# One-core two-layer hybrid encoder: moving loads, copies and token updates at the border between the layers

## The chip, the cores and the metric

The kernel runs on one core of a Trainium2 chip. The metric is the device time of one execution in microseconds; the median of the runs is quoted. Engines: TensorE (PE) multiplies, VectorE (DVE) and ScalarE (ACT) do elementwise work, GpSimd (POOL) does small work and issues stores, SyncE (SP) issues loads. Each engine works through its own queue in order.

## The reference

Two layers of a hybrid block over 512 tokens of width 2048, in float32:

```
h = rmsnorm(x, g_pre)
z = h @ w_in                     # 2048 -> 7184 columns: GLA q,k,v,gate,alpha and attention q,k,v,gate
o_gla = gated linear attention (4 heads, chunk 64), rmsnorm per head, * silu(gate)
o_att = chunked attention with relative bias (8 heads), rmsnorm per head, * silu(gate)
y = concat(o_gla, o_att) @ w_out # 2048 -> 2048
x = x + rmsnorm(y, g_post)
```

The change touches the end of the first layer's output projection (`w_out`), the update of `x`, and the start of the second layer's input projection.

## The kernel before

**Matrix products.** Weights are cut into blocks of 512 columns. A float32 product is made of three products of parts: each operand is split into a high part and the rest, and high times high, high times low and low times high are added up. For a weight chunk (128 x 1024) `Job.high` makes the high part with a ScalarE cast (line 202, tile `wh`, four buffers), `Job.low` the low part with a VectorE subtraction (line 211, tile `wl`, three buffers). Token operands are split in the same way (lines 105 and 106).

The gate blocks (`AG0`, `AG1`) are multiplied directly (`std_gemm`, line 311): eight chunks, and for two token tiles 12 matmuls per chunk. All other blocks are multiplied in pairs by a seven-product scheme (`fast_gemm`, lines 379 and 389): products P1 to P7 with four chunks each, 12 matmuls per chunk. Their weights are sums of quarter blocks built in a tile `H`: P1 takes H as loaded, P5, P6 and P4 add a loaded `raw` chunk to H (line 196), P7 takes H minus a chunk (line 198), P2 and P3 take `raw` chunks. The output projection consists of the pairs W01 and W23; their order is `PROD_END`: P1 and P2 alternately, then P5 and P6, P3, P7, P4.

**Preparing ahead.** All chunks of both layers stand in one list. After each chunk `ahead()` issues loads up to five, casts and low parts up to four chunks ahead. A scheduler with a model of the engines turns the program into one queue per engine; `tc.issue_after(i)` ties the instructions in its block behind instruction i, where both stand on the same engine. `last_load`, `last_h`, `last_cast`, `last_low` are the latest load, H load, cast and low part.

**The border.** `project` (line 1317) takes the outputs of a product, squares them on ScalarE with a running sum (line 1330), and multiplies them with the gain `g_post` on VectorE (line 1334, or 1343 for W01's, late). For W01's last product P4 it first copies them from the accumulator (line 1328). When one half of the tokens is complete, `finish_both` (line 1368) reduces the squares, takes the power -1/2 on POOL (line 431), and updates x: z = y * r + x, on VectorE (line 1386), each stored to `x_mid` by POOL. The first half is complete after P7 of W23, the second after P4. `prep_half` then squares the new rows (line 444), reduces (445), takes the power, scales the rows (ScalarE line 499, VectorE line 501), transposes them on TensorE (515), evacuates with the next layer's gain (526), and splits them into operands `a11c`, `a12c` and others.

The old x rows are loaded by `Tokens.load` (line 459) a piece at a time from `residual`, during W23. Updates of the second half stand behind chosen splits (`half_lows`), and P4's sums in W23 of the first layer behind chosen updates (`half_adds`).

Of the kernel before, what the change touches and what calls it, by code (L numbers as in the profile page):

```python
# [16 lines left out]
L = 2  # L17
S = 512
D = 2048
# [14 lines left out]
def hybrid_trunk(  # L34
# [104 lines left out]
    class Job:  # L139
# [14 lines left out]
        def load(self):  # L154
            k, c, p, b0, b1 = self.kind, self.c, self.pair, self.b0, self.b1
            end = b0 >= NB_IN and k != "std"
            if end:
                c = OC[c]
            top, bottom = (c + 4, c) if end else (c, c + 4)
            if k == "std":  # L160
                self.raw = self.fetch(rtile("raw", bufs=5), b0, c)
            elif k == "P1":
                p["H", self.c] = self.fetch(rtile("H"), b0, top)
                last_h[0] = last_load[0]
            elif k == "P5":
                p["r", self.c] = self.fetch(rtile("raw", bufs=5), b1, top)
            elif k == "P6":
                p["r", self.c] = self.fetch(rtile("raw", bufs=5), b1, bottom)
            elif k == "P7":
                p["r", self.c] = p.pop(("t", self.c), None) or self.fetch(rtile("raw", bufs=5), b0, top)  # L170
            elif k == "P2" or (k == "P4" and end):
                p["r", self.c] = self.fetch(rtile("raw", bufs=5), b0, bottom)
            sums = (so_d if end else sa_d)[self.l]
            src = sums.get((LEFT.get(k), c))
            if src is not None and b0 != NB_IN and not (k == "P5" and b0 == AV0):
                until(lambda: k == "P4" or (id(sums), LEFT[k], c) in written)
                self.a = rtile("sa", (2, 512), F32R)
                last_load[0] = nc.sync.dma_start(flat(self.a), src).ins
            if k == "P5" and b0 == W23[0] and self.l == L - 1:
                with tc.issue_after(last_h[0]):  # L180
                    p["t", self.c] = self.fetch(slot(SPARE[self.c], [2, 512]), b0, c + 4)

        def high(self):
# [3 lines left out]
            else:  # L187
                h, r = p["H", c], p.get(("r", c))
                src = h if k in ("P1", "P5", "P6", "P4") else r
                with ExitStack() as ties:  # L190
                    if self.b0 >= NB_IN:
                        ties.enter_context(tc.issue_after(lows[-2]))
                    if k == "P4" and self.l < L - 1 and self.b0 == W23[0]:
                        ties.enter_context(tc.issue_after(half_adds[3 if self.c else 1]))
                    if k in ("P5", "P6") or (k == "P4" and self.b0 >= NB_IN):
# [288 lines left out]
    full = {}  # L484
    half_adds, half_lows, half_turns, half_rows = [], [], [], [None]

# [236 lines left out]
    def layer(l):  # L723
# [595 lines left out]
        def project(o, n, src, gp=None, comb=None, between=None):  # L1319
# [6 lines left out]
            y = src if comb is None else comb(dst if gp is None else t2())  # L1326
            if gp is None and comb is None:
                nc.scalar.copy(dst, src)
            j = t2(dtype=BF16)
            nc.scalar.activation(j, y, AF.Square, scale=D ** -0.5, accum_out=ssy[o][:, n : n + 1])  # L1330
            if between is not None:
# [38 lines left out]
        def finish_both(pair, xs):  # L1370
# [6 lines left out]
            yield  # L1377
            n = 0
            for j in range(2):
                t, c0 = 2 * pair + j, 0  # L1380
                for z in xs[j]:
                    wd = z.shape[-1]
                    yt = ys[t, c0 // 1024][:, c0 % 1024 : c0 % 1024 + wd]
                    with tc.issue_after(half_lows[3 + n // 2]) if pair else nullcontext():
                        half_adds.append(
                            nc.vector.scalar_tensor_tensor(
                                out=z, in0=yt, scalar=r[:, j : j + 1], in1=z, op0=ALU.mult, op1=ALU.add
                            ).ins
                        )
                    nc.gpsimd.dma_start(x_mid[t * P : (t + 1) * P, c0 : c0 + wd], z)  # L1390
                    n, c0 = n + 1, c0 + wd
                    if c0 % 1024 == 0:
                        yield

# [47 lines left out]
        def residual(k, c):  # L1442
# [71 lines left out]
```

## Time and profile before

| | |
|---|---|
| median of 3 runs (lowest, highest) | 1627.13 us (1626.03, 1629.71) |
| profiled execution: its own time, its span | 1630.47 us, 1628.4 us |
| TensorE, weight load, VectorE, ScalarE, POOL busy | 1605.2, 1374.1, 1271.8, 919.2, 128.9 us |
| mean granted TensorE clock | 0.996 |
| read from and written to device memory | 377.02 MB, 61.62 MB; 269 GB/s over the span |

W23 of the first layer starts at 728 us of the span, its P4 at 795, the second layer at 813. In the rows of instructions the first number is the start in us from the start of the span, the second the time from the start of the first to the end of the last instruction of the row, "x3" their count, and in brackets the engine's idle time before it and what ended that. Waits are in us in total, how often, and the longest. In the stretches, each engine has its busy time and instructions; then come the granted TensorE clock, the DMA engines' busy share and GB/s.

### The profile page before, as it was taken

What the parts mean: (1) busy time and instruction counts of PE and PEld (TensorE: products, weight loads), DVE (VectorE), ACT (ScalarE), POOL (GpSimd) and SP (SyncE); (2) the same over time, 40 slices, a digit from 0 to 9 for tenths busy, and PEclk for the clock granted to TensorE, in tenths of its full rate; (3) what the DMA queues carried; (4) which work ended last, traced back from release to release, by engine and by line L of the source; (5) the groups of instructions that cost most, each with busy time, mean ns of one, the idle gap of its engine ahead of it and who ended that gap; (6) DMA issues with size and microseconds to landing.
All of it is one profiled execution on the core that took longest, in us unless ns stands there. A gap on an engine that the chain in (4) does not pass through costs nothing.

```text
span 1628.4 us, 24480 instructions
## 1 busy us (share of the span) xinstructions
PE 1605.2 (99%) x8938; PEld 1374.1 (84%) x8938; DVE 1271.8 (78%) x1646; ACT 919.2 (56%) x1507; POOL 128.9 (8%) x192
## 2 busy tenths in 40 slices
PE   9999999999999999999989999999999999999997
PEld 7887999998888778878778889999988887788886
DVE  5987778678677868988878677686786778689887
ACT  7544445566555556665686444456574555565644
POOL 0120000010000010100122000000100100101001
PEclk9999999999999999999999999999999999999999
DMA  9697686785868768697879976866958677686887
GB/s 370 235 386 265 239 296 209 230 304 175 278 215 296 249 227 302 229 345 262 305 240 336 377 248 247 285 229 223 314 212 282 214 282 267 219 305 239 330 301 196
DMA packets 133928, 438.17 MB, mean 269 GB/s; under 512 B 14404, under 2 KB 27204, under 8 KB 133776
## 3 DMA queue, kind: packets, MB, share of 16 engines
q1 hardware_dynamic: 117072, 375.99, 66.4%
q0 software_dynamic: 16160, 59.53, 9.9%
q8 instruction: 71, 1.16, 0.3%
q10 hardware_dynamic: 576, 1.08, 0.2%
q14 instruction: 49, 0.40, 0.1%
HBM read 377.02 MB, written 61.62 MB: 269 GB/s over the span
## 4 chain that ended last, share of the span: by engine, by line
PE 89%; DVE 3%; DMA 3%; issue 2%; ACT 1%; POOL 0%; DVEq 0%; SPq 0%; POOLq 0%; ACTq 0%
PE mm L389 49%; PE mm L379 20%; PE mm L311 8%; PE ax L939 2%; PE ax L389 2%; DMA raw<-in_w_dram 1%; PE ax L1125 1%; PE ax L922 1%; DVE wl L211 1%; PE ax L1097 1%; PE ax L902 1%; PE ax L901 1%; PE ax L900 1%; DMA H<-in_w_dram 1%; DMA S<-g 1%
## 5 line engine op out<-in xcount | busy, mean ns | idle before, releaser
L389 PE MATMUL mm<-wh,sa 128*128 128x512 f32 x1600 | 518.0, 394 | 1.8 <-DMA sa<-S 0.9
L211 DVE TENSOR_TENSOR wl<-H,wh 128x1024 fp32r<-128x1024 f32 x256 | 312.1, 1220 | 98.7 <-PE mm L389 31.7
L202 ACT CAST wh<-H 128x1024 fp32r<-128x1024 f32 x256 | 268.4, 1051 | 212.0 <-PE mm L389 89.7
L389 PEld LDWEIGHTS mm<-wh,sa 128*128 128x128 f32 x1600 | 299.4, 188 | 74.6 <-issue 9.7
L202 ACT CAST wh<-raw 128x1024 fp32r<-128x1024 f32 (+1 forms) x237 | 248.5, 1052 | 200.9 <-PE mm L389 90.4
L211 DVE TENSOR_TENSOR wl<-raw,wh 128x1024 fp32r<-128x1024 f32 (+1 forms) x237 | 287.6, 1216 | 68.1 <-PE mm L389 27.1
L389 PE MATMUL mm<-wl,sa 128*128 128x512 f32 x800 | 312.6, 391 | 0.3 <-DVE wl L211 0.3
L379 PE MATMUL mm<-sa,wh 128*128 128x256 f32 x1280 | 237.4, 285 | 0.0
L389 PE MATMUL mm<-wh,a 128*128 128x512 f32 x640 | 211.5, 394 | 2.1 <-ACT wh L202 2.1
L379 PEld LDWEIGHTS mm<-sa,wh 128*128 128x128 f32 x1280 | 200.2, 191 | 0.3
L379 PE MATMUL mm<-sa,wl 128*128 128x256 f32 x640 | 181.1, 283 | 0.0
L389 PEld LDWEIGHTS mm<-wl,sa 128*128 128x128 f32 x800 | 150.3, 188 | 30.3 <-DVE wl L211 0.7
L196 DVE TENSOR_TENSOR H<-H,raw 128x1024 f32<-128x1024 f32 x144 | 174.9, 1219 | 1.0
L389 PEld LDWEIGHTS mm<-wh,a 128*128 128x128 f32 x640 | 119.3, 188 | 27.7 <-ACT wh L202 2.9
L389 PE MATMUL mm<-wl,a 128*128 128x512 f32 x320 | 125.7, 393 | 0.0
L379 PEld LDWEIGHTS mm<-sa,wl 128*128 128x128 f32 x640 | 122.5, 191 | 0.3 <-DVE wl L211 0.2
L198 DVE TENSOR_TENSOR raw<-H,raw 128x1024 f32<-128x1024 f32 x60 | 73.5, 1224 | 51.9 <-DMA raw<-in_w_dram 51.6
L431 POOL TENSOR_TENSOR sm<-sm,mhalf 128x2 f32<-128x2 f32 (+2 forms) x40 | 53.0, 1324 | 762.5 <-DVE sm L949 459.2
L389 PE MATMUL mm<-wh,g 128*128 128x512 f32 x320 | 101.7, 391 | 1.5 <-ACT ev L341 1.2
L379 PE MATMUL mm<-a,wh 128*128 128x256 f32 x512 | 95.4, 285 | 0.0
L341 ACT COPY ev<-mm 128x512 f32<-128x512 f32 x104 | 60.8, 585 | 60.6 <-PE mm L389 43.9
L217 DVE TENSOR_TENSOR H<-H,raw 128x1024 f32<-128x1024 f32 x48 | 58.7, 1224 | 38.2 <-DMA raw<-in_w_dram 38.1
(247 smaller groups left out, 2316.2 us busy)
## 6 DMA issues: line engine op xcount, KB each, us to landing
raw<-in_w_dram SPq DMA_DIRECT2D x315, 512.0 KB, 5.2
sa<-S SPq DMA_DIRECT2D x184, 512.0 KB, 4.4
H<-in_w_dram SPq DMA_DIRECT2D x64, 512.0 KB, 5.1
sa<-A SPq DMA_DIRECT2D x48, 512.0 KB, 5.8
S<-g POOLq DMA_DIRECT2D x32, 512.0 KB, 9.6
sa<-oS SPq DMA_DIRECT2D x32, 512.0 KB, 5.5
oS<-g POOLq DMA_DIRECT2D x16, 512.0 KB, 4.5
oS<-sa POOLq DMA_DIRECT2D x16, 512.0 KB, 5.7
```

The costliest lines, as they stand in the source:

```text
L196: nc.vector.tensor_tensor(out=h, in0=h, in1=r, op=ALU.add)
L198: nc.vector.tensor_tensor(out=r, in0=h, in1=r, op=ALU.subtract)
L202: last_cast[0] = nc.scalar.copy(self.wh[:, z, :], src[:, z, :]).ins
L211: last_low[0] = nc.vector.tensor_tensor(out=self.wl[:, z, :], in0=self.src[:, z, :], in1=self.wh[:, z, :].bitcast(F32), op=ALU.subtract).ins
L217: nc.vector.tensor_tensor(out=h, in0=h, in1=self.src, op=ALU.add)
L311: nc.tensor.matmul(pss[o], a(part, kk, o) if callable(a) else a[:, part, t], rhs[:, kk, :], start=(i == 0 and kk == 0 and m == 0), stop=(i ...
L341: nc.scalar.copy(e, src[t])
L379: nc.tensor.matmul(dst, lhs[:, kk, f], a[:, part, tok], start=(fresh and kk == 0 and m == 0 and ft % 2 == 0), stop=(c == 3 and kk == 1 and ...
L389: last_mm[0] = nc.tensor.matmul(out_ps[t], a[:, part, tok], rhs[:, kk, :], start=(fresh and kk == 0 and m == 0), stop=(c == 3 and kk == 1 ...
L431: nc.gpsimd.tensor_tensor(out=out_r, in0=v, in1=mhalf[:, : v.shape[-1]], op=ALU.pow)
L900: nc.tensor.matmul(ps[:, :n], self.qh[:, t], self.kh[:, :n], start=True, stop=False)
L939: nc.tensor.matmul(o, self.pt[i][:, j * P : (j + 1) * P], av[hd // 4, j // 2][:, j % 2, (hd % 4) * P : (hd % 4 + 1) * P], start=(j == 0), ...
```

## The change

Five edits, all at the end of an output projection.

1. `finish_both`: the second half's six updates are tied behind the latest low part (`last_low`) instead of behind chosen splits, and the task yields after each update (before: after each full row piece of 1024 columns). The list `half_adds` goes.
2. `high`: P4's sums in the first layer's W23 are no longer tied behind updates.
3. `residual`: x loads are tied behind the latest H load instead of the latest load of any kind. Operand loads (`sa`) of W23 in the first layer (`mid`) are tied behind the latest H load too.
4. `load`: in the first layer's W23, P7's own chunks are fetched when P6 is prepared, into the slots `a110` to `a113`, which hold P1's operands until P1 is done. Before, they were fetched into the `raw` ring when P7 was prepared. The second layer has an early fetch already, at P5.
5. `project`: the ScalarE copies (and squares) of W01's P4 are tied behind the latest cast.

```diff
@@ load
+            mid = end and b0 == W23[0] and self.l < L - 1
...
             if src is not None and b0 != NB_IN and not (k == "P5" and b0 == AV0):
                 until(lambda: k == "P4" or (id(sums), LEFT[k], c) in written)
                 self.a = rtile("sa", (2, 512), F32R)
-                last_load[0] = nc.sync.dma_start(flat(self.a), src).ins
-            if k == "P5" and b0 == W23[0] and self.l == L - 1:
+                with tc.issue_after(last_h[0]) if mid else nullcontext():
+                    last_load[0] = nc.sync.dma_start(flat(self.a), src).ins
+            if b0 == W23[0] and k == ("P6" if mid else "P5"):
                 with tc.issue_after(last_h[0]):
-                    p["t", self.c] = self.fetch(slot(SPARE[self.c], [2, 512]), b0, c + 4)
+                    p["t", self.c] = self.fetch(slot(f"a11{self.c}" if mid else SPARE[self.c], [2, 512]), b0, c + 4)
@@ high
-                with ExitStack() as ties:
-                    if self.b0 >= NB_IN:
-                        ties.enter_context(tc.issue_after(lows[-2]))
-                    if k == "P4" and self.l < L - 1 and self.b0 == W23[0]:
-                        ties.enter_context(tc.issue_after(half_adds[3 if self.c else 1]))
+                with tc.issue_after(lows[-2]) if self.b0 >= NB_IN else nullcontext():
@@ project
-            if gp is None and comb is None:
-                nc.scalar.copy(dst, src)
             j = t2(dtype=BF16)
-            nc.scalar.activation(j, y, AF.Square, scale=D ** -0.5, accum_out=ssy[o][:, n : n + 1])
+            with tc.issue_after(last_cast[0]) if gp is None and comb is None else nullcontext():
+                if gp is None and comb is None:
+                    nc.scalar.copy(dst, src)
+                nc.scalar.activation(j, y, AF.Square, scale=D ** -0.5, accum_out=ssy[o][:, n : n + 1])
@@ finish_both
-            n = 0
...
-                    with tc.issue_after(half_lows[3 + n // 2]) if pair else nullcontext():
-                        half_adds.append(
-                            nc.vector.scalar_tensor_tensor(
-                                out=z, in0=yt, scalar=r[:, j : j + 1], in1=z, op0=ALU.mult, op1=ALU.add
-                            ).ins
+                    with tc.issue_after(last_low[0]) if pair else nullcontext():
+                        nc.vector.scalar_tensor_tensor(
+                            out=z, in0=yt, scalar=r[:, j : j + 1], in1=z, op0=ALU.mult, op1=ALU.add
                         )
                     nc.gpsimd.dma_start(x_mid[t * P : (t + 1) * P, c0 : c0 + wd], z)
-                    n, c0 = n + 1, c0 + wd
-                    if c0 % 1024 == 0:
-                        yield
+                    c0 += wd
+                    yield
@@ residual
-                xs[half].load(last_load[0], 1)
+                xs[half].load(last_h[0], 1)
```

The queues that come out differ in the first layer's W23 and the first blocks of the second layer, and in a few places at the second layer's W23. Line numbers of the changed kernel are one to three lower than before (the low part is at 209, the update at 1383).

**Start of W23, first layer.** ScalarE's queue; `g8` and `g11` take W01's last outputs from the accumulators `mm_1266` and `mm_1267`, `H_1373` and `H_1387` are P1's first two chunks, `raw_1384` and `raw_1390` P2's. Before:

```order
L1330 ACTIVATE t2_1378_7199,ssy_1376_7195<-g8_1377_7197 128x512
L1330 ACTIVATE t2_1381_7205,ssy_1379_7201<-g11_1380_7203 128x512
L1328 COPY g8_1377_7197<-mm_1266_6621 128x512
L1330 ACTIVATE t2_1394_7280,ssy_1376_7195<-mm_1266_6621 128x512
L202 CAST wh_1383_7221<-H_1373_7189 128x1024
L202 CAST wh_1386_7239<-raw_1384_7223 128x1024
L1328 COPY g11_1380_7203<-mm_1267_6622 128x512
```

Now:

```order
L200 CAST wh_1383_7221<-H_1373_7189 128x1024
L1329 ACTIVATE t2_1378_7199,ssy_1376_7195<-g8_1377_7197 128x512
L1329 ACTIVATE t2_1381_7205,ssy_1379_7201<-g11_1380_7203 128x512
L200 CAST wh_1386_7239<-raw_1384_7223 128x1024
L200 CAST wh_1389_7257<-H_1387_7241 128x1024
L200 CAST wh_1392_7275<-raw_1390_7259 128x1024
L1328 COPY g8_1377_7197<-mm_1266_6621 128x512
```

The four casts of the first two P1 and P2 chunks stand ahead of the copies. On SP's queue, before, the H loads stand among operand loads (`sa`) and x loads (`g16`, `g17`, `g12`):

```order
L178 DMA sa_1428_7421<-oS202_128 128x1024
L151 DMA raw_1390_7259<-in_w_dram 128x1024
L459 DMA g17_1422_7396<-in_x_dram 128x1024
L151 DMA raw_1404_7309<-in_w_dram 128x1024
L151 DMA H_1373_7189<-in_w_dram 128x1024
L178 DMA sa_1432_7444<-oS100_122 128x1024
L459 DMA g12_1423_7397<-in_x_dram 128x1024
L151 DMA raw_1412_7349<-in_w_dram 128x1024
L151 DMA H_1387_7241<-in_w_dram 128x1024
L151 DMA raw_1415_7369<-in_w_dram 128x1024
L151 DMA H_1393_7277<-in_w_dram 128x1024
L151 DMA H_1409_7330<-in_w_dram 128x1024
```

Now:

```order
L151 DMA H_1373_7189<-in_w_dram 128x1024
L151 DMA raw_1412_7349<-in_w_dram 128x1024
L151 DMA H_1387_7241<-in_w_dram 128x1024
L151 DMA raw_1415_7369<-in_w_dram 128x1024
L151 DMA H_1393_7277<-in_w_dram 128x1024
L151 DMA H_1409_7330<-in_w_dram 128x1024
L180 DMA sa_1416_7371<-oS102_124 128x1024
L180 DMA sa_1420_7393<-oS103_125 128x1024
L457 DMA g16_1421_7395<-in_x_dram 128x1024
L180 DMA sa_1428_7421<-oS202_128 128x1024
L457 DMA g17_1422_7396<-in_x_dram 128x1024
```

All four H loads go first; four operand loads (two of them stand ahead of the rows shown before) and three x loads follow.

**From P7 to P4 of W23.** VectorE's queue: `wl_1504` is the low part of P7's last chunk, `H_1373` to `H_1409` are P4's four chunks, `wl_1512` and `wl_1522` P4's first two low parts; line 1386, now 1383, is the first half's update. Before:

```order
L1386 SCALAR_TENSOR_TENSOR g16_1421_7395<-a122_1326_6929,sm_1503_7754,g16_1421_7395 128x1024
L1386 SCALAR_TENSOR_TENSOR g17_1422_7396<-g0_1439_7472,sm_1503_7754,g17_1422_7396 128x1024
L196 TENSOR_TENSOR H_1373_7189<-H_1373_7189,raw_1497_7741 128x1024
L1386 SCALAR_TENSOR_TENSOR g12_1423_7397<-a123_1329_6935,sm_1503_7754,g12_1423_7397 128x1024
L1386 SCALAR_TENSOR_TENSOR g13_1424_7398<-g1_1442_7478,sm_1503_7754,g13_1424_7398 128x1024
L196 TENSOR_TENSOR H_1387_7241<-H_1387_7241,raw_1506_7779 128x1024
L445 TENSOR_REDUCE sm_1507_7785<-sm_1509_7787 128x1
L211 TENSOR_TENSOR wl_1512_7806<-H_1373_7189,wh_1505_7777 128x1024
```

Now (P4's first two sums stand further ahead, each before a line 1333):

```order
L209 TENSOR_TENSOR wl_1504_7774<-a113_1466_7562,wh_1496_7739 128x1024
L194 TENSOR_TENSOR H_1387_7241<-H_1387_7241,raw_1506_7779 128x1024
L1333 TENSOR_TENSOR g1_1444_7482<-t2_1500_7748,t2_1397_7287 128x512
L1372 TENSOR_REDUCE sm_1502_7753<-ssy_1328_6933 128x1
L209 TENSOR_TENSOR wl_1512_7806<-H_1373_7189,wh_1505_7777 128x1024
L194 TENSOR_TENSOR H_1393_7277<-H_1393_7277,raw_1514_7811 128x1024
L1383 SCALAR_TENSOR_TENSOR g16_1421_7395<-a122_1326_6929,sm_1503_7754,g16_1421_7395 128x1024
L1383 SCALAR_TENSOR_TENSOR g17_1422_7396<-g0_1441_7476,sm_1503_7754,g17_1422_7396 128x1024
L1383 SCALAR_TENSOR_TENSOR g12_1423_7397<-a123_1329_6935,sm_1503_7754,g12_1423_7397 128x1024
L1383 SCALAR_TENSOR_TENSOR g13_1424_7398<-g1_1444_7482,sm_1503_7754,g13_1424_7398 128x1024
L209 TENSOR_TENSOR wl_1522_7841<-H_1387_7241,wh_1513_7809 128x1024
```

P4's first low part and three of its sums go ahead of the updates, its second low part behind all four.

**First block of the second layer (AG0).** VectorE's queue: `raw_1564` and `raw_1567` are AG0's chunks 3 and 4, `a112` is the operand that chunk 4 multiplies. Before:

```order
L211 TENSOR_TENSOR wl_1575_8065<-raw_1564_8019,wh_1566_8035 128x1024
L1334 TENSOR_TENSOR g3_1541_7909<-mm_1401_7292,t2_1396_7285 128x512
L1373 TENSOR_REDUCE sm_1573_8054<-ssy_1379_7201 128x1
L106 TENSOR_TENSOR a112_1548_7933<-H_1547_7930,a112_1548_7933 128x512
L106 TENSOR_TENSOR a122_1550_7943<-H_1547_7930,a122_1550_7943 128x512
L106 TENSOR_TENSOR a113_1556_7972<-H_1555_7969,a113_1556_7972 128x512
L1386 SCALAR_TENSOR_TENSOR g9_1449_7506<-g8_1377_7197,sm_1574_8055,g9_1449_7506 128x1024
L1386 SCALAR_TENSOR_TENSOR g10_1450_7507<-g2_1538_7903,sm_1574_8055,g10_1450_7507 128x1024
...
L211 TENSOR_TENSOR wl_1578_8087<-raw_1567_8037,wh_1576_8067 128x1024
```

(Left out: the four half-width updates.) Now:

```order
L209 TENSOR_TENSOR wl_1575_8065<-raw_1564_8019,wh_1566_8035 128x1024
...
L106 TENSOR_TENSOR a111_1532_7877<-H_1531_7874,a111_1532_7877 128x512
L106 TENSOR_TENSOR a121_1545_7922<-H_1531_7874,a121_1545_7922 128x512
L1383 SCALAR_TENSOR_TENSOR g9_1451_7510<-g8_1377_7197,sm_1574_8055,g9_1451_7510 128x1024
L1383 SCALAR_TENSOR_TENSOR g10_1452_7511<-g2_1538_7903,sm_1574_8055,g10_1452_7511 128x1024
L209 TENSOR_TENSOR wl_1578_8087<-raw_1567_8037,wh_1576_8067 128x1024
L1383 SCALAR_TENSOR_TENSOR sg_1453_7512<-g11_1380_7203,sm_1574_8055,sg_1453_7512 128x512
L1383 SCALAR_TENSOR_TENSOR sg_1454_7513<-g11_1380_7203,sm_1574_8055,sg_1454_7513 128x512
L1383 SCALAR_TENSOR_TENSOR bias_1455_7514<-g3_1541_7909,sm_1574_8055,bias_1455_7514 128x512
L106 TENSOR_TENSOR a112_1548_7933<-H_1547_7930,a112_1548_7933 128x512
L209 TENSOR_TENSOR wl_1581_8111<-raw_1577_8069,wh_1579_8089 128x1024
```

Chunk 4's low part stands behind two of the updates, and the low part of its operand behind five of them. On ScalarE the cast of chunk 3 now stands ahead of the last four pairs of evacuations (line 526), before it stood behind them.

More of the change, by code (lines that the diff above doesn't have):

```diff
@@ L484, in hybrid_trunk @@
     full = {}
-    half_adds, half_lows, half_turns, half_rows = [], [], [], [None]
+    half_lows, half_turns, half_rows = [], [], [None]
     def prep_half(l, half, xs):
```

## Prediction

> **What bounds the kernel now.** I read the page's first part, then the chain of waits, then the waits of TensorE alone, then TensorE's instructions in order of time around each wait. The first part and one row of the chain:
>
> ```profile
> PE 1605.2 (99%) x8938; PEld 1374.1 (84%) x8938; DVE 1271.8 (78%) x1646; ACT 919.2 (56%) x1507; POOL 128.9 (8%) x192
> ...
> 1564.07 54.41 PE mm L389 x240
> ```
>
> TensorE is busy for 99% of the span, and the chain lies on it. Undisturbed, 240 matmuls take 54.41 us: 0.227 us each, 2.72 us for the 12 of a chunk. The change takes no matmul away, so it can only win time in which TensorE stands still or runs slowly. The waits of TensorE over the whole span (us in total, times, longest):
>
> ```profile
> PE mm L311 <- DVE wl L211: 5.1, 1, 5.1
> PE mm L389 <- ACT wh L202: 2.8, 5, 1.5
> PE mm L389 <- DVE wl L211: 1.3, 2, 1.1
> PE mm L389 <- ACT ev L341: 1.2, 2, 1.0
> ```
>
> Nearly all of it falls between 726 and 835 us, at the border of the layers. TensorE there, in order of time (start, us, idle before):
>
> ```profile
> 726.39 0.39 PE L389 MATMUL mm<-wh,g 128*128 128x512 f32 x1
> 728.30 0.73 PE L389 MATMUL mm<-wh,a 128*128 128x512 f32 x2 [1.52 <-ACT wh L202]
> ...
> 734.36 0.62 PE L389 MATMUL mm<-wh,a 128*128 128x512 f32 x2
> ...
> 781.20 0.47 PE L389 MATMUL mm<-wh,sa 128*128 128x512 f32 x1 [0.41 <-DMA sa<-oS]
> ...
> 794.69 0.39 PE L389 MATMUL mm<-wh,sa 128*128 128x512 f32 x1
> ...
> 798.38 0.50 PE L389 MATMUL mm<-wl,g 128*128 128x512 f32 x1 [1.06 <-DVE wl L211]
> ...
> 812.87 0.39 PE L311 MATMUL mm<-wh,a 128*128 128x512 f32 x1
> ...
> 823.56 0.84 PE L311 MATMUL mm<-wh,a 128*128 128x512 f32 x3
> 829.51 0.79 PE L311 MATMUL mm<-wl,a 128*128 128x512 f32 x1 [5.12 <-DVE wl L211]
> ...
> 834.79 0.40 PE L311 MATMUL mm<-wl,a 128*128 128x512 f32 x1
> ```
>
> Four losses, each against the pitch of 0.227 us. **A**, start of W23: the next matmul was due at 726.62 and came at 728.30 (1.68); the 24 from there to 734.36 took 6.06 where 5.44 are due (0.62); 2.30 in all. **B**: 0.42 at 781.20. **C**, first P4 chunk: due at 794.92; two matmuls squeeze in, the third is due at 795.37 and comes at 798.38: 3.01. **D**, chunk 4 of the next layer's first block (AG0): due at 824.25, comes at 829.51 (5.26); then twelve matmuls take until 834.79, 5.28 instead of 2.72: 2.56 more, 7.82 in all. That these twelve ran slowly is seen in the granted clock, the last column but two of the stretches:
>
> ```profile
> 820.00:830.00 10.00, 4.88 (x21) 3.80 (x20) 10.00 (x15) 10.00 (x21) 4.45 (x10) 0.90 0.60 215
> 830.00:840.00 10.00, 10.00 (x35) 7.95 (x35) 9.09 (x20) 3.79 (x10) 1.53 (x1) 0.76 0.85 271
> ```
>
> A + B + C + D = 13.55 us: all that these edits could win. The same columns show VectorE and ScalarE busy for all ten microseconds before the wait, so what counts is the order in which they do their work.
>
> **The edits, part by part.** *A: copies behind casts, x loads behind H loads.* What ends the wait in A:
>
> ```profile
> 715.53 0.40 SPq L151 DMA_DIRECT2D H<-in_w_dram  x1
> ...
> 720.88 0.33 SPq L151 DMA_DIRECT2D H<-in_w_dram  x1
> ```
> ```profile
> 726.13 0.59 ACT L1328 COPY g<-mm 128x512 f32<-128x512 f32 x1 [4.74 <-PE mm L389]
> ...
> 727.20 1.04 ACT L202 CAST wh<-H 128x1024 fp32r<-128x1024 f32 x1
> ```
> ```profile
> raw<-in_w_dram SPq DMA_DIRECT2D x25, 512.0 KB, 6.5
> H<-in_w_dram SPq DMA_DIRECT2D x4, 512.0 KB, 10.2
> ```
>
> ScalarE stands 4.74 us before a copy that needs TensorE's last product, and the cast that TensorE needs next is queued behind it. H was there: issued at 715.53, landed 10.2 later, at 725.7. The second H landed at 731.1. In the new order the first cast stands ahead of the copies, and two more chunks' casts after it; nothing is queued behind the copies that W23 needs before its P5 chunks, some 20 us later. Three x loads and four operand loads (0.5 MB each) leave the place ahead of the H loads on SP's queue, so the H loads, released by the low parts of W01's last chunks, should land as the raw loads do, after about 6.5, by 722; even the second, issued as late as before, would be there at 727.4 and is wanted at 732. A falls to 0; if the second H were still late, 0.6 would stay. I take 0, because 4.6 us of room lie between.
>
> *P7's chunks fetched at P6; x loads earlier.* B is an operand load that landed late in a stretch full of loads. About 2 MB of x and 2 MB of P7's chunks now move ahead of it. B to 0, from 0 to 0.4. The new loads wait on SP for slots that P1's operands free; behind them stand loads for P6. The order also lets the P2 outputs (four half-width operations, 2.4 us) pass ahead of the P6 sums on VectorE, in a stretch where TensorE now waits for nothing: 0 to 0.6 new, taken as 0.3. Cover here is the chunk or two that casts run ahead.
>
> *C: no tie on P4's sums.* VectorE and its prices:
>
> ```profile
> 784.19 0.68 DVE L346 TENSOR_TENSOR t<-mm,ev 128x512 f32<-128x512 f32 x1
> ...
> 789.98 1.29 DVE L1386 SCALAR_TENSOR_TENSOR g<-a,sm,g 128x1024 f32<-128x1024 f32 x1 [0.90 <-POOL sm L431]
> ...
> 797.10 1.22 DVE L211 TENSOR_TENSOR wl<-H,wh 128x1024 fp32r<-128x1024 f32 x1
> ...
> 819.59 1.23 DVE L211 TENSOR_TENSOR wl<-raw,wh 128x1024 fp32r<-128x1024 f32 x1 [0.91 <-ACT wh L202]
> ...
> 821.39 1.89 DVE L106 TENSOR_TENSOR a<-H,a 128x512 fp32r<-128x512 f32 x3
> 823.20 2.47 DVE L1386 SCALAR_TENSOR_TENSOR g<-g,sm,g 128x1024 f32<-128x1024 f32 x2
> 825.59 1.41 DVE L1386 SCALAR_TENSOR_TENSOR sg<-g,sm,sg 128x512 f32<-128x512 f32 x2
> ...
> 828.24 1.22 DVE L211 TENSOR_TENSOR wl<-raw,wh 128x1024 fp32r<-128x1024 f32 x1
> ...
> 829.98 2.35 DVE L211 TENSOR_TENSOR wl<-raw,wh 128x1024 fp32r<-128x1024 f32 x2
> ```
>
> Successive low parts (or sums) stand 1.14 apart (2.35 less 1.22), half-width ones 0.60, updates 1.2 and 0.67. Before, P4's first low part began at 797.10, behind four updates. Count from 794.92, when TensorE wants P4. VectorE starts this stretch at 784.19, that is -10.7. The new order has, up to P4's third sum, six full-width and four half-width operations: 9.3, so to -1.4, with P4's first low part done at -2.5: in time. TensorE loses 0.3 because the copies that free its accumulators stand behind three casts. Then the four updates (4.8, to 3.4) and P4's second low part (to 4.6); TensorE wants it at 0.3 + 14 x 0.227 = 3.5: 1.1 lost. C: 1.4 instead of 3.0. Were the updates to go first again 3.0 stay, without any wait 0.
>
> What is late next is the first half's rows. The squares end at about 5.6, VectorE's reductions at 7.0, then a power on POOL, then two scalings on ScalarE:
>
> ```profile
> L431 POOL TENSOR_TENSOR sm<-sm,mhalf x4: 712/1300/2760, 789.2 to 832.5; 128x2 f32<-128x2 f32 x4
> ```
> ```profile
> 802.40 2.19 ACT L499 ACTIVATE g<-g,sm 128x1024 f32<-128x1024 f32 x2 [1.86 <-POOL sm L431]
> ```
>
> The power takes 0.71 to 2.76; the rows are ready at 8.9 to 10.9 and 10.0 to 12.0. TensorE, now with P4's third chunk ahead of the transposes, asks at 4.6 + 22 x 0.227 = 9.6, and for the second row 0.5 later: 0 to 1.9 new, taken as 1.0.
>
> *D: updates one per step.* Six updates stood in one block before chunk 4's low part. Now two stand ahead of it and three between it and the low part of its operand, which TensorE's fifth matmul of the chunk needs. From the end of chunk 3's low part: three half-width operations and a reduction 1.9, two updates 2.4, low part 1.14, three short updates 2.0, operand 0.6: 8.0, and 0 to 1.8 for POOL: as long as before (819.59 to 829.4). But before, chunk 3's low part began at 819.59 though chunk 0, whose buffer it takes, was multiplied by 812.87 + 2.72 = 815.6: it waited for its cast, behind ScalarE's evacuations of the second transposes. In the new order that cast is ahead of them. From the end of chunk 0, VectorE needs 0.1 + 1.14 + 8.0 to 9.8 = 9.2 to 11.0, TensorE 40 x 0.227 = 9.1. Wait 0.1 to 1.9, taken as 1.1. Waits of 1.52 and 1.06 left the clock at full in the rows above, so nothing is added. D: 1.1 instead of 7.82; if the cast stays 3.9 late, about 5 and the slow clock.
>
> On POOL two small memsets change places with stores; what they feed is reduced later in both orders: 0. In W01 of the second layer the same copies move; TensorE waits 0.3 at most there: 0.
>
> **Sum**: left over or new 0.3 + 1.4 + 1.0 + 1.1 = 3.8; gain 13.55 - 3.8 = 9.7. The span of 1628.4 becomes 1618.7, this execution 1630.47 becomes 1620.8. The execution shown lies 3.3 above the median of the runs (1627.13), which becomes **1617.4**.
>
> **Rivals.** *1, VectorE becomes the bound.* Before, VectorE was through with the second half's rows well ahead and then stood waiting for TensorE:
>
> ```profile
> 843.14 1.23 DVE L211 TENSOR_TENSOR wl<-raw,wh 128x1024 fp32r<-128x1024 f32 x1 [2.07 <-PE mm L311]
> ```
>
> It has the same 50 us of work from 784 on; TensorE comes 8 us sooner and eats that cushion. If POOL takes its 2.76 both times and casts come 2 late, C stays at 3.0, the transposes wait 1.9, D waits 3.5 and the clock drops (2.56): 11.3 left, gain 2 to 6, middle 4: 1623. For it: both engines are full there. Against: the new order has the casts earlier. [...]
>
> *2, the order on paper does not hold.* The updates are still in clumps of two and three, and the loads were hidden but for B. Then only A and B come: 2.7, less 0.3 to 2 new: gain 0 to 2.7, 1625.5. Against: A to D are different places with causes of their own.
>
> *3, slower: the queue of SP.* A wait there holds everything behind it:
>
> ```profile
> SPq L151 <- DVE wl L211: 115.6, 44, 10.8
> ```
>
> The fetches for P7 wait for P1's matmuls, two x loads for the last use of the gains; behind them stand P6's operands. P6's second chunk is the thirteenth of W23, wanted 12 x 2.72 = 33 us after its start, and a load lands in 6.5. It costs from the point where the last slot or gain comes free later than 26 us after the start; P1's last chunk, the seventh, is done after 19. Were SP held until 31, four chunks would each wait 4 to 5 with the slow clock once, some 16 us, against 13.5 to be won: 1630. [...]
>
> **How the numbers follow.** Forecast 0.70 (gain 6 to 13.5), rival 1 0.14, rival 2 0.09, rival 3 0.07. 0.2% (3.3 us) is about what can be told from no change: faster is below 1623.9. The forecast and three quarters of rival 1 are below (0.70 + 0.11, and a little of rival 2): 0.83; within 0.10; slower 0.07. The forecast's own range is 1613.6 (nothing new) to 1621; reaching into rival 1, 1614 to 1624.
>
> **What would show it.** Right: no wait of TensorE over 2 us between 720 and 840; clock 1.00 there; no ScalarE copy ahead of W23's first cast; H landing in about 6.5; AG0's chunk 4 about 9 us earlier. A wait at the first transposes would be the POOL term. Wrong: a wait over 3 us with a clock below 0.95, or TensorE waiting for operand loads between 745 and 770.

## The result, and the profile after

The changed kernel takes 1617.15 us (median of 4 runs, 1615.87 to 1619.0), the kernel before 1628.42 (4 runs beside them): a ratio of 0.9928, 95% interval 0.9908 to 0.9947, which is 11.7 us less (8.6 to 15.0). 1617.4 was forecast. The execution profiled took 1617.52 with a span of 1615.5.

The page's first part, and the waits of TensorE over the whole span (us in total, times, longest):

```profile
PE 1600.5 (99%) x8938; PEld 1372.8 (85%) x8938; DVE 1272.4 (79%) x1646; ACT 918.5 (57%) x1507; POOL 131.5 (8%) x192
```
```profile
PE mm L387 <- DVE wl L209: 1.2, 1, 1.2
PE ax L674 <- DVE t L671: 1.2, 1, 1.2
PE mm L309 <- ACT wh L200: 1.0, 1, 1.0
...
PE ax L513 <- ACT g L497: 0.4, 1, 0.4
```

The wait of 5.1 is gone, and so are those of 1.5 and 0.4. The second and third rows lie at the program's start (1.2 and 6.4 us), so what the border still costs is in the first and the last. TensorE at the border, in order of time (start, us, idle before):

```profile
790.92 0.40 PE L387 MATMUL mm<-wh,g 128*128 128x512 f32 x1
...
792.08 1.09 PE L387 MATMUL mm<-wh,g 128*128 128x512 f32 x3
...
795.74 0.50 PE L387 MATMUL mm<-wl,g 128*128 128x512 f32 x1 [1.19 <-DVE wl L209]
...
801.03 0.65 PE L513 MATMUL ax<-cst,g 128*128 128x128 f32 x4
802.07 1.53 PE L513 MATMUL ax<-cst,g 128*128 128x128 f32 x12 [0.38 <-ACT g L497]
...
807.87 0.47 PE L309 MATMUL mm<-wh,a 128*128 128x512 f32 x1
...
819.32 0.61 PE L309 MATMUL mm<-wl,a 128*128 128x512 f32 x2
820.08 0.72 PE L309 MATMUL mm<-wh,a 128*128 128x512 f32 x2
```

And TensorE by stretches (us busy, matmuls; the granted clock in the last column but two):

```profile
720.00:740.00 20.00, 20.00 (x90) 16.57 (x89) 14.00 (x15) 11.80 (x19) 0.00 (x0) 1.00 1.03 408
820.00:830.00 10.00, 9.92 (x44) 8.20 (x45) 9.37 (x15) 8.62 (x16) 2.66 (x4) 1.00 0.93 312
830.00:840.00 10.00, 10.00 (x56) 8.49 (x55) 7.54 (x15) 8.46 (x21) 1.39 (x2) 1.00 0.81 304
```

**A** is 0: TensorE is busy for all 20 us around the start of W23. **B** is 0: no wait for an operand load. **C** is 1.6: P4 starts on time at 790.92, its fifteenth matmul is due 14 x 0.227 = 3.2 later, at 794.1, and comes at 795.74; 0.25 of it lies in the three matmuls at 792.08, 1.4 in the wait for the low part. The first transposes lose 0.5 (0.2 ahead of them; the 16 then take 2.3 us where they took 2.0). **D** is 0.3: chunk 4's first matmul with its low part, which came at 829.51, comes 10.2 us earlier, at 819.32, and only the chunk's fifth matmul, at 820.08, is late. Together 2.4, where 13.55 stood before, and the clock stays at 1.00 where it had been 0.90 and 0.76.

The border thus gives 11.1 of the 12.9 us between the two spans. Another 1.2 was there before the border is reached (a wait for a cast that stands at 685.95 in the one trace stands at 684.74 in the other), where the change moves nothing. That much is the scatter of executions: over the traces of all kernels shown here, this wait stands between 683.48 (copy_alone) and 686.94 (loads_alone). A difference of two spans is therefore no measure of an edit; the losses at the border and the medians are. The last 0.6 is not placed.

### The profile page after: what moved, and what is told of

Read it like the earlier page. It is cut to its first block, busy times and chain, and to the rows that moved or that the text cites. A ratio compares the mean times of both kernels' runs of the same rounds, so it can differ in the third digit from the quotient of the medians.

```text
span 1615.5 us, 24476 instructions
## 1 busy us (share of the span) xinstructions
PE 1600.5 (99%) x8938; PEld 1372.8 (85%) x8938; DVE 1272.4 (79%) x1646; ACT 918.5 (57%) x1507; POOL 131.5 (8%) x192
## 4 chain that ended last, share of the span: by engine, by line
PE 94%; DVE 2%; DMA 1%; issue 1%; ACT 1%; POOL 0%; DVEq 0%; SPq 0%; ACTq 0%; POOLq 0%
PE mm L387 53%; PE mm L377 19%; PE mm L309 10%; PE ax L937 2%; PE ax L387 2%; PE ax L1123 1%; PE ax L920 1%; PE ax L744 1%; PE ax L1095 1%; DMA raw<-in_w_dram 1%; PE ax L900 1%; PE ax L899 1%; PE ax L898 1%; DVE wl L209 0%; DMA bias<-in_rel_dram 0%
## 5 line engine op out<-in xcount | busy, mean ns | idle before, releaser
L200 ACT CAST wh<-raw 128x1024 fp32r<-128x1024 f32 (+1 forms) x233 | 244.1, 1052 | 197.0 <-PE mm L387 89.5
L209 DVE TENSOR_TENSOR wl<-raw,wh 128x1024 fp32r<-128x1024 f32 (+1 forms) x233 | 282.4, 1215 | 61.9 <-PE mm L387 24.5
L196 DVE TENSOR_TENSOR raw<-H,raw 128x1024 f32<-128x1024 f32 x56 | 68.5, 1223 | 51.1 <-DMA raw<-in_w_dram 50.5
```

The source lines that it names most:

```text
L196: nc.vector.tensor_tensor(out=r, in0=h, in1=r, op=ALU.subtract)
L200: last_cast[0] = nc.scalar.copy(self.wh[:, z, :], src[:, z, :]).ins
L209: last_low[0] = nc.vector.tensor_tensor(out=self.wl[:, z, :], in0=self.src[:, z, :], in1=self.wh[:, z, :].bitcast(F32), op=ALU.subtract).ins
```

## The experiments

Each kernel was timed against the kernel before on the same chip. "Less" is one minus the ratio, times 1629 us. Line numbers of the experiments lie a few above or below those of the changed kernel.

| kernel | median us | less than before, us (95%) |
|---|---|---|
| the change | 1617.15 | 11.7 (8.6 to 15.0) |
| vec_alone | 1622.02 | 7.2 (5.1 to 9.5) |
| no_vec | 1618.02 | 10.4 (8.3 to 12.4) |
| no_loads | 1617.85 | 10.9 (8.8 to 12.9) |
| no_copy | 1617.22 | 11.7 (9.6 to 13.7) |
| copy_alone | 1623.26 | 6.7 (4.7 to 8.8) |
| loads_alone | 1625.25 | 3.9 (2.6 to 5.4) |
| updates_alone | 1626.13 | 3.6 (2.1 to 5.0) |
| no_p7 | 1617.19 | 11.7 (9.8 to 13.8) |
| no_upd | 1618.00 | 11.2 (9.3 to 13.0) |
| tie_alone | 1621.62 | 6.4 (4.4 to 8.3) |
| low_first | 1620.44 | 8.3 (6.4 to 10.3) |
| vector_load | 1620.72 | 8.0 (6.0 to 9.9) |

### VectorE's two edits alone, and all but them

**vec_alone** is the kernel before with these two edits only; **no_vec** is the changed kernel without them:

```diff
-                    if k == "P4" and self.l < L - 1 and self.b0 == W23[0]:
-                        ties.enter_context(tc.issue_after(half_adds[3 if self.c else 1]))
...
-                    with tc.issue_after(half_lows[3 + n // 2]) if pair else nullcontext():
+                    with tc.issue_after(last_low[0]) if pair else nullcontext():
...
-                    if c0 % 1024 == 0:
-                        yield
+                    yield
```

> The kernel before with only the two edits of VectorE's order: no tie on P4's sums, and the updates one per step behind low parts. Loads, P7's fetches and ScalarE's copies stay as before. My theory: C and D are won here alone, C 3.0 to 1.4, D 7.8 to 0.3, the first transposes then wait 0.7: 8.4 us less than before, with A (1.7 and 0.6) and B (0.4) still to be seen as waits, and TensorE's clock at 1.00 in AG0. Rival (the order on paper does not hold, the loads and casts carry the gain): 0 to 1 us less than before, the wait of 5 us in AG0 still there.

> The changed kernel with these same two edits undone: loads, P7's fetches and copies as in the change, VectorE's order as before. My theory: only A and B are won, 2.7 us less than before (2 to 3.5), and the wait of about 5 us with half-speed matmuls behind it stands again in AG0's chunk 4. Rival (the earlier casts of the other edits make AG0's chunk 4 early by themselves): 7 to 10 us less than before, no wait over 2 us in AG0.

The first came out near its figure (7.2 for 8.4), with A and B still there. The second did not: without the two edits 10.4 us are still won, and the rival on record, that the other edits make AG0's chunk 4 early by themselves, holds. TensorE in no_vec, then ScalarE there:

```profile
793.14 0.50 PE L391 MATMUL mm<-wl,g 128*128 128x512 f32 x1 [1.06 <-DVE wl L213]
...
823.21 0.50 PE L313 MATMUL mm<-wl,a 128*128 128x512 f32 x1 [0.15 <-DVE wl L213]
```
```profile
810.31 1.07 ACT L204 CAST wh<-raw 128x1024 fp32r<-128x1024 f32 x1
...
811.84 3.05 ACT L528 ACTIVATE H<-ax,gcol 128x256 f32<-128x256 f32 x8
```

C is as before; D is 0.15, and that at chunk 5. The first row of ScalarE is the cast of AG0's chunk 3: it stands ahead of the eight evacuations of the second transposes. Before, it stood behind all eight. So 7.2 and 10.4 together are far more than the 11.7 of both: the two groups of edits win the same thing, D. The prediction had named that cast as what made D short. The next runs ask whether it is the cast's place or the updates' places.

### One edit at a time

Four kernels, each the one before with one edit. **tie_alone** takes the tie off P4's sums (the first two lines of the diff above), **updates_alone** has the rest of that diff. **copy_alone** ties the copies behind casts, **loads_alone** the x loads and W23's operand loads behind the H loads:

```diff
+            with tc.issue_after(last_cast[0]) if gp is None and comb is None else nullcontext():
                 if gp is None and comb is None:
                     nc.scalar.copy(dst, src)
```
```diff
+                with tc.issue_after(last_h[0]) if mid else nullcontext():
                     last_load[0] = nc.sync.dma_start(flat(self.a), src).ins
...
-                xs[half].load(last_load[0], 1)
+                xs[half].load(last_h[0], 1)
```

In tie_alone and copy_alone the cast of chunk 3 comes ahead of the second transposes' evacuations, in the other two it stays behind them.

> The kernel before with one edit alone: ScalarE's last copies of W01 behind casts. In its order, far behind that place, the cast of AG0's chunk 3 comes ahead of the evacuations of the second transposes, and chunk 4's low part stands between the updates, though nothing was said of the updates. Theory now (the late cast was the cause of D, and any edit that pulls it ahead wins D): A 2.3 to 1.7 and D 7 to 7.8 won, C 3.0 stays: 8 to 10 us less than before. Rival (the updates one per step and behind low parts removed D): only A is won, 1.5 to 2.5 us less than before, and the wait of 5 us stays.

> The kernel before with the x loads and operand loads of W23 behind the H loads, and nothing else. H lands in about 6, the first casts of W23 come ahead of the copies: A is won. In its order the cast of AG0's chunk 3 still stands behind the second transposes' evacuations, with six updates in one block before chunk 4's low part. Theory of the late cast: D 7.8 and C 3.0 stay, 2 to 4 us less than before (the upper end if the clock sometimes drops in A), with a wait of about 5 us in AG0. Rival (the earlier start of TensorE or the loads undid D): 8 to 10 us less than before.

> The kernel before with the updates one per step behind low parts, and P4's tie kept. In its order the cast of AG0's chunk 3 is as late as before; chunk 4's low part stands behind two updates, and three updates behind it ahead of the operand that the fifth matmul needs. Theory of the late cast: chunk 4's low part ends at about 826.8 instead of 829.4, its operand at 829.4 as before, so TensorE waits about 2.5 and then 1.7: D 4.2 instead of 7.8, if the clock holds 3.6 us less than before, and if it drops 1 to 2 less. Rival (the updates' places removed D): 7 us less than before, no wait over 2 us in AG0.

> The kernel before with one edit alone: no tie on P4's sums. P4's first low part moves ahead of the four updates, and in the order as it falls out the cast of AG0's chunk 3 comes ahead of most of the second transposes' evacuations. Theory: C 3.0 to about 1.6, D gone or under 2, A and B stay: 6 to 9 us less than before, about the same as the two edits together measured (7.3 less). Rival (this edit is worth C alone): 1 to 2 us less.

TensorE's longest wait in AG0 in copy_alone, in loads_alone and in updates_alone; tie_alone has none there (its stretch is the last fence):

```profile
825.25 0.49 PE L312 MATMUL mm<-wl,a 128*128 128x512 f32 x1 [1.70 <-DVE wl L212]
```
```profile
826.98 0.75 PE L313 MATMUL mm<-wl,a 128*128 128x512 f32 x1 [3.94 <-DVE wl L213]
```
```profile
826.25 0.61 PE L312 MATMUL mm<-wl,a 128*128 128x512 f32 x1 [2.48 <-DVE wl L212]
```
```profile
820.00:830.00 10.00, 10.00 (x46) 8.29 (x45) 9.65 (x15) 10.00 (x22) 2.61 (x6) 1.00 0.94 308
```

With the late cast chunk 4 waits for its low part, with the early one it does not (the 1.70 of copy_alone is chunk 5's), whatever the edits say of the updates. loads_alone shows how the late cast works, on ScalarE and then on VectorE, which stands idle for it in a stretch where it is otherwise full:

```profile
813.03 3.05 ACT L528 ACTIVATE H<-ax,gcol 128x256 f32<-128x256 f32 x8
815.89 1.13 ACT L204 CAST wh<-raw 128x1024 fp32r<-128x1024 f32 x1
```
```profile
817.05 1.23 DVE L213 TENSOR_TENSOR wl<-raw,wh 128x1024 fp32r<-128x1024 f32 x1 [1.96 <-ACT wh L204]
```

But the cast is not the only thing that differs. In every kernel with the early cast, chunk 4's low part also stands behind two updates only, even where the updates' edit is not made (copy_alone, tie_alone, no_vec); before and in loads_alone it stands behind all six. VectorE in no_vec, then in updates_alone, the one kernel with two updates ahead and the cast late:

```profile
814.55 2.48 DVE L1389 SCALAR_TENSOR_TENSOR g<-g,sm,g 128x1024 f32<-128x1024 f32 x2 [0.81 <-POOL sm L443]
816.95 1.22 DVE L213 TENSOR_TENSOR wl<-raw,wh 128x1024 fp32r<-128x1024 f32 x1
```
```profile
822.59 2.47 DVE L1386 SCALAR_TENSOR_TENSOR g<-g,sm,g 128x1024 f32<-128x1024 f32 x2
824.98 1.22 DVE L212 TENSOR_TENSOR wl<-raw,wh 128x1024 fp32r<-128x1024 f32 x1
```

So the updates' places alone bring the wait from 5.12 to 2.48, and the rest goes with the cast. An early cast with all six updates ahead of the low part was not run: that the cast would do it by itself is argued, not shown.

updates_alone met its wait (2.5 was worked out, 2.48 came) and its upper figure (3.6 less), but not in the way expected: the second wait of 1.7 did not come, and the twelve matmuls from 826.25 on took 4.44 instead of 2.72, the first eight of them at about half speed (0.42 us each instead of 0.227, the granted clock 0.83 over 820 to 830), which costs the same 1.7. tie_alone (6.4 for 6 to 9) and loads_alone (3.9 for 2 to 4, with a wait of 3.94 where about 5 was expected) came out as their theory says. copy_alone won less than the 8 to 10 expected. Its trace shows where: A keeps 1.0 of 2.30, since H still lands late and TensorE waits 0.20 and 0.22 for casts; the operand load is late by 0.71; and D keeps 1.9, because TensorE now comes sooner than the low part of chunk 5, which stands behind four short updates.

### The changed kernel less one edit

**no_loads** and **no_copy** take the lines of the last two diffs out again, **no_upd** those of the updates, and **no_p7** P7's fetches:

```diff
-            if b0 == W23[0] and k == ("P6" if mid else "P5"):
+            if k == "P5" and b0 == W23[0] and self.l == L - 1:
```

> The changed kernel with the x loads and operand loads of W23 put back to where they were, ahead of the H loads; the copies stay behind casts. My theory: H lands about 10 us after its issue again, at 725 to 726, the cast follows at once and TensorE waits 0.2 to 0.5 for it, and about 0.6 for the second H: 0.5 to 1.5 us slower than the changed kernel, so about 10 to 11 us less than before. Rival (only the copies were the cause of A, the loads were hidden): the changed kernel's time within 0.3 us.

> The changed kernel with ScalarE's last copies of W01 not tied behind casts; the loads stay as in the change. In the order as it then stands one cast of W23 falls behind the first copy, not the first one. My theory, as I now read the order: the first cast is early because H lands early, the tie moves only the second or third cast, and TensorE waits 0 to 0.5: the changed kernel's time within 0.5 us. Rival (as the prediction has it, the copies ahead of the cast were what held TensorE): 1.5 us of A come back, about 1.5 us slower than the changed kernel.

> The changed kernel with P7's chunks formed in the raw ring by VectorE again instead of fetched at P6 (four low-priority subtractions of 1.14 us come back, four loads of 0.5 MB go). My theory: B was a single late operand load; with the x loads already out of the way it does not come back: the changed kernel's time within 0.6 us, a wait for an operand load of 0 to 0.4 us between 760 and 785. Rival (the four fetches carry part of the gain, since they take 4.6 us from VectorE ahead of P4): 1 to 3 us slower than the changed kernel, with P4's first low part late.

> The changed kernel with the updates' old tie and steps put back (two per step, behind the gate block's half low parts); P4's sums stay untied, loads and copies as in the change. In its order the cast of AG0's chunk 3 stays early, and two short updates stand behind each operand instead of three ahead of it. Theory of the late cast: the updates' own edit carries nothing, the time is the changed kernel's within 0.7 us, and TensorE waits under 0.5 at chunk 4. Rival (the updates one per step are what removed D, as the prediction's part on D has it): 3 to 8 us slower than the changed kernel.

None of the four can be told from the changed kernel (nor can no_vec, whose interval of 8.3 to 12.4 holds 11.7). In no_loads, H is late again, and ScalarE stands waiting for it, but TensorE does not (issues and their median time to landing; ScalarE):

```profile
H<-in_w_dram SPq DMA_DIRECT2D x4, 512.0 KB, 10.2
```
```profile
723.21 1.05 ACT L199 CAST wh<-H 128x1024 fp32r<-128x1024 f32 x1 [3.06 <-DMA H<-in_w_dram]
...
728.33 1.05 ACT L199 CAST wh<-H 128x1024 fp32r<-128x1024 f32 x1 [3.12 <-DMA H<-in_w_dram]
```

The first cast starts as H lands, at 723.21, and TensorE takes its product at 725.38. Since nothing else is queued ahead of the casts, 10.2 is early enough. With the loads early instead and the copies untied (no_copy), the first cast is done before the copies can start. So the early loads remove A without the tie on the copies (loads_alone has no wait there either), and the tie does it here without the early loads. With the late loads it is close: I had expected no_loads to give back 0.5 to 1.5, and it gave back nothing that can be measured, but in copy_alone, where TensorE came 1.2 us sooner (it wanted the product at 724.15, the cast ended at 724.46), A kept 1.0.

no_p7 has no operand load late, and neither has no_loads, so either of the two edits is enough against B. Of the five traces with the old loads and without P7's fetches four have a late operand load (0.41 before, 0.42 in vec_alone, 0.71 in copy_alone, 0.16 in updates_alone); of the nine with at least one of the two edits, one (low_first, 0.25).

### How much room VectorE has

**low_first** puts P4's second low part ahead of the last update; **vector_load** computes chunk 4's low part three times:

```diff
+            base = len(lows)
+            while not pair and len(lows) < base + 2:
+                yield
...
-                    last_low[0] = nc.vector.tensor_tensor(
+                    for _ in range(3 if (self.l, self.b0, self.c) == (1, AG0, 4) else 1):
+                        last_low[0] = nc.vector.tensor_tensor(
```

> The changed kernel with P4's second low part put ahead of the last of the first half's four updates; everything else the same up to there. TensorE's wait of 1.19 for that low part falls to 0. My theory: VectorE sets the pace from there to the first half's rows, so the last update and with it the rows come 1.2 later, and the wait comes back at the first transposes (0.7 becomes 2 to 3): the changed kernel's time within 1 us. Rival (the 1.2 is slack that an order can win): 1.0 to 1.5 us faster than the changed kernel.

> The changed kernel with chunk 4's low part of AG0 computed three times over, so that VectorE has 2.3 us more to do ahead of it. It asks how much room VectorE has in AG0 (the first rival of the prediction). In the changed kernel the low part is ready 1.6 us before TensorE takes it and its fifth matmul's operand is 0.3 late. If VectorE sets the pace there: TensorE waits 2 to 2.6 more, 1617 becomes 1619 to 1620, and up to 2.5 more where the clock drops behind the wait. If VectorE had room (it idles again at 838): the changed kernel's time within 0.5 us.

TensorE in low_first, then in vector_load:

```profile
798.31 0.50 PE L387 MATMUL mm<-wl,g 128*128 128x512 f32 x1 [0.45 <-DVE wl L209]
803.14 0.66 PE L513 MATMUL ax<-cst,g 128*128 128x128 f32 x4 [2.27 <-ACT g L497]
```
```profile
810.82 1.02 PE L310 MATMUL mm<-wh,a 128*128 128x512 f32 x2 [1.81 <-DVE a L106]
```

In low_first the wait of 1.19 shrank to 0.45 at a later low part, and 2.27 came back at the first transposes; the whole is 3.4 us worse than the change, more than the 1 I had allowed. Not all of the 2.27 is VectorE's. The power on POOL ahead of the rows, in the changed kernel and then in low_first:

```profile
798.17 1.62 POOL L429 TENSOR_TENSOR sm<-sm,mhalf 128x2 f32<-128x2 f32 x1 [2.79 <-DVE sm L443]
```
```profile
799.08 2.83 POOL L429 TENSOR_TENSOR sm<-sm,mhalf 128x2 f32<-128x2 f32 x1 [2.26 <-DVE sm L443]
```

It started 0.9 later and took 1.2 longer. Its length went with the order: 1.62 in all eight traces in which P4's sums are untied and the four updates stand together, 2.75 or 2.76 in all five in which the sums are tied. What makes it so, the traces don't show. So low_first does not settle whether another order could win the 1.19.

In vector_load 2.3 us of work on VectorE cost 3.7 (8.0 less than before instead of 11.7): a wait of 1.81 and about half speed behind it (nine matmuls at 0.42 us each, the granted clock 0.83 over 810 to 820). The load fell on another place than I meant: the chunk that the program numbers 4 is the second that AG0 multiplies, not the fifth, and what came late was an operand of the first. AG0 is also multiplied twice, once for each half of the tokens, so VectorE got the two extra low parts twice (1650 instructions instead of 1646); the second time, at 858, TensorE waited for nothing. Ahead of AG0's first chunk, then, VectorE has no room; its idle time at 838 comes too late to be any. What room there is at the fifth chunk was not measured.

## Why the prediction was right, point by point

**A to 0: right.** The H loads land in 6.0 (6.5 was worked out) and the first casts stand ahead of the copies, on ScalarE:

```profile
719.57 1.05 ACT L200 CAST wh<-H 128x1024 fp32r<-128x1024 f32 x1 [1.39 <-DMA H<-in_w_dram]
...
722.89 1.05 ACT L200 CAST wh<-H 128x1024 fp32r<-128x1024 f32 x1
726.02 1.06 ACT L200 CAST wh<-raw 128x1024 fp32r<-128x1024 f32 x1 [2.08 <-PE mm L387]
726.98 0.57 ACT L1328 COPY g<-mm 128x512 f32<-128x512 f32 x1
```

What the prediction did not see is that the two edits named for A do the same thing: with the early loads the tie on the copies is spare (no_copy, loads_alone), and with the tie the late loads cost 0 (no_loads) to 1.0 (copy_alone).

**B to 0: right** in the sum. Two edits were named for it, and either is enough; with both in place a late load of 0.25 still came once, in low_first.

**C to 1.4: right**, 1.6: the 0.3 for the accumulators' copies came as 0.25, the 1.1 for the second low part behind the four updates as 1.4. The one order that was tried against it, low_first, was slower.

**First transposes 1.0: 0.5**, with a power on POOL of 1.62, inside the 0.71 to 2.76 of the rows.

**D to 1.1: 0.3**, and the reason given is right in the main, though not the edit under whose heading it stood. The part on D worked out that the updates' new places leave VectorE's sum "as long as before", 8.0 us, and put the gain on the cast of chunk 3 ahead of the evacuations; with the cast late it gave "about 5 and the slow clock". updates_alone is that case, and loses 4.4: 2.64 at the wait and 1.72 at half speed. So the cast goes with more than half of D, and the places with the other 3.5, which the prediction had at almost nothing. no_upd lost nothing, but its order too has only two updates ahead of the low part. The row of the cast after the change is at 809.07, ahead of the evacuations:

```profile
809.07 1.09 ACT L200 CAST wh<-raw 128x1024 fp32r<-128x1024 f32 x1
...
812.34 2.36 ACT L524 ACTIVATE H<-ax,gcol 128x256 f32<-128x256 f32 x6
```

Which edit moves that cast, the prediction left unsaid. Two do it each by itself: the tie taken from P4's sums and the tie put on the copies, both far ahead of the place. Loads alone and updates alone don't. Loads together with fetches were not tried alone, and no run undoes the tie on P4's sums alone.

**The sum** was too cautious by 1.4: 3.8 left over was forecast, 2.4 stands. That the time was met all the same (1617.15 for 1617.4) is in part luck. The gain was 9.7 forecast and 11.7 measured; the forecast went by the three runs shown, 1627.13, and with a fourth the median before is 1628.42, with the 9 to 21 runs beside the experiments 1628.5 to 1629.3. Between the medians the gain is 11.3, so a gain 1.6 too small met a start 1.3 too low.

**A step that was wrong**: "Waits of 1.52 and 1.06 left the clock at full in the rows above, so nothing is added." They did in that one execution. In others the same waits were followed by about half speed (a granted clock of 0.91 over 720 to 740 in vec_alone, of 0.83 over 790 to 800 in no_vec), at 1.6 us each, so "nothing is added" was in part luck for the waits that the change leaves: in the one trace of the changed kernel the 1.19 was not followed by a drop. It also means that the losses removed may be worth more, on average, than the one profile showed. That this is where the missing gain came from is not shown: 1.4 of it is the sum above.

**The rivals.** Rival 1 (VectorE as the bound) is true of the place and did not come: VectorE's cushion is used up, as vector_load shows, but the order leaves just enough. Rival 1's sum charges a wait of 3.5 with slow matmuls of 2.56; no run shows that term. Behind waits of 1.81, 2.48 and 3.94 the slow matmuls cost 1.7 each (in loads_alone eight, from 826.98 on, took 3.52 instead of 1.82), behind 1.70 and 2.27 nothing. Rival 2 (the order does not hold) is out by the rows above. Rival 3 (SP's queue) is out: TensorE waits for no load at the border.

No experiment beats the change. no_copy and no_p7 equal it with one edit less each.

## What to carry to other kernels

When several edits each aim at their own stall, find by single undos what each is worth: here four edits that win 6.4, 6.7, 3.9 and 3.6 us alone win 11.7 together with a fifth, not 20.6, because several removed the same stalls. Then look at the order that each undo leaves: an edit to one place moved instructions in others, so that an undo of the updates' edit did not put the updates back. A stall that names VectorE can be due in part to one late ScalarE instruction before it, as in loads_alone, where VectorE stood 1.96 us for a cast ahead of TensorE's wait of 3.94; look at what the waiting engine itself stood waiting for in the ten microseconds before. And when a wait of one or two microseconds is priced from a profile, read the granted clock behind it in more than one execution.

## What the runs showed of the hardware

The same wait is followed by a drop of TensorE's clock in one execution and not in another. At the start of W23, four kernels leave the old order in place, with the same waits of 1.52 and 0.2 one after the other. The stretch 720 to 740 of the kernel before and of tie_alone, then of vec_alone and of updates_alone:

```profile
720.00:740.00 20.00, 18.27 (x79) 14.49 (x79) 11.26 (x14) 10.53 (x17) 0.00 (x0) 1.00 0.91 353
```
```profile
720.00:740.00 20.00, 18.27 (x79) 14.47 (x78) 11.21 (x13) 10.25 (x14) 0.00 (x0) 1.00 0.90 346
```
```profile
720.00:740.00 20.00, 18.27 (x72) 14.31 (x71) 9.80 (x11) 10.01 (x17) 0.00 (x0) 0.91 0.90 352
```
```profile
720.00:740.00 20.00, 18.27 (x73) 14.28 (x72) 10.19 (x11) 9.80 (x14) 0.00 (x0) 0.91 0.82 315
```

TensorE was busy for the same 18.27 us and did 79 matmuls in two of them and 72 or 73 in the others. In vec_alone, 24 matmuls took 7.69 us from 728.49 on, where the kernel before needed 6.06: 1.6 us more. At the first P4 chunk, waits of 1.0 and 1.1 left the clock at 1.00 in the kernel before, in copy_alone and in updates_alone, and were followed by 0.83 in no_vec and loads_alone; the row of copy_alone, then of no_vec:

```profile
790.00:800.00 10.00, 7.73 (x32) 5.58 (x32) 9.39 (x12) 7.35 (x13) 4.00 (x4) 1.00 0.96 338
```
```profile
790.00:800.00 10.00, 7.92 (x27) 5.88 (x26) 9.39 (x12) 7.39 (x11) 4.61 (x4) 0.83 0.99 337
```

In no_vec, nine matmuls from 793.94 to 797.58 took 3.64 us instead of 2.04. Among single waits, 2.48 (updates_alone, a clock of 0.83 over 820 to 830), 3.94 (loads_alone, 0.85) and 5.12 (before, 0.90, then 0.76) were followed by a drop and so was the 1.81 of vector_load (0.83 over 810 to 820), while 1.70 (copy_alone) and 2.27 (low_first) were not, nor the 1.19 of the changed kernel, in its own trace and in those of the four less one edit (1.17 to 1.19): the clock is 1.00 in all of these stretches. In these traces the length of a wait alone does not decide. How much of the scatter of single times comes from it is open: one execution of each kernel was traced, and the traces differ by up to 3.5 us ahead of the border already.

Nor does the sum of two waits: the two at the start of W23, 1.73 or 1.74 us within 2.5 us, were followed by a drop in two of the four executions. What decides it, the traces don't show, and no run here set out to find it.
